# A decoder layer on one core: PSUM as four single banks and two pairs, with small products in groups of a pair

## The chip, the cores and the metric

The kernel runs on one core of one Trainium2 chip. The metric is the device time of one execution in microseconds (us), as the median of several runs. The engines are TensorE (PE; its weight loads are PEld), VectorE (DVE), ScalarE (ACT), GpSimd (POOL) and SyncE (SP), which here only issues DMAs. TensorE writes its results into PSUM, eight banks of 512 fp32 columns on each of 128 partitions; VectorE and ScalarE read them from there.

## The reference

One layer of a decoder works on x, 256 tokens of width 2048, in fp32:

```python
x = x + 0.5 * swiglu(rms_norm(x, g1), w_gate1, w_up1, w_down1)      # width 5632
p = rms_norm(x, g) @ w_in
# sliding-window attention: 16 heads of 64 in 4 key groups, blocks of 128 tokens
s = where(valid, (q @ k.T) * 64 ** -0.5, -1e30)
m = maximum(max(s, -1), sink)
e = exp(s - m)
y_attn = (e / (sum(e, -1) + exp(sink - m))) @ v
# RWKV-7: 16 heads of 64, a recurrence over the tokens, on p and p shifted by one token
y_rwkv = rwkv7_time_mix(p_rwkv, ...)
x = x + (gate_a * (y_attn @ w_proj_attn) + gate_r * (y_rwkv @ w_proj_rwkv)) @ w_out
x = x + softmax(q2 @ km.T * 128 ** -0.5) @ vm @ w_cross_o           # 4 heads, 256 memory rows
x = x + 0.5 * swiglu(rms_norm(x, g2), w_gate2, w_up2, w_down2)
out = rms_norm(x, g_final)
```

## The kernel before

**Weights and products.** A weight matrix comes from memory in pieces of 512 KB (128 partitions x 1024 columns, two blocks of 128 rows). `split_raw` (L315) makes two fp32r parts of each piece: `hi`, a cast on ScalarE (L321), and `lo`, the rest, a subtraction on VectorE (L322). The activations are split in the same way. `times` (L406) makes one product of a weight block as three products of 128x128 by 512 columns, one after the other, into one bank: hi by hi (L409), lo by hi (L410), hi by lo (L411). `product` (L387) runs these over all blocks for the two halves of the tokens. w_in has 17 column blocks of 512 and one of 288, whose pieces are 128x576 and whose products are 288 columns wide.

**Seven products.** In the feed-forward nets `product_pair` (L467) works two column blocks of 512 for both halves of the tokens. For some of the row blocks (SEVEN, SEVEN_DOWN) it makes them with seven products, p1 to p7, in place of eight, from sums of weights (`sums`, L334: first operation L341, then the parts thi at L346 and tlo at L347) and sums of activations (`combinations`, L421). For the others it uses p2, p4, p3 and p5 (p8 in w_down) as plain accumulators. `gate_up` (L526) and `down` (L557) give what is done when a sum is complete: `after(b)` reads p1, `end(b)` reads p6, p7 and p5 (L534 to L536), `finish` reads p2, p4, p3 and p5 (L542 to L550; p3 and p5 by the line L549). `gate_up` is called 20 times, in groups that w_down follows.

**PSUM.** The eight banks are three pools of tiles: `acc` (three), `mm` (three) and `tr` (two), each tile one bank (L164 to L171). A tile is given out in the order in which the code asks for it; the next user of a bank waits until the last reader of the tile before it is done. Dependencies are tracked by tile.

**Small products.** Between weight products TensorE makes small ones of 64 to 128 rows: transposes by `feat` (L599: four of 128x128 into one bank, then a copy or split of 512 columns by `split`, L609 with the lines L611 and L612, `to_features`, L847, or `Norm.block`, L626), the scores, transposes and value products of attention, and the products of the recurrence in chunks of 128 tokens (`invert` L1206, `chain` L1290 with `masked` L1315, `finish` L1420).

**Attention.** `attend(kv, qb)` (L857) handles one key group and one block of 128 queries, so there are eight units. Each makes its scores in two mm banks (L179, `by_turns`), adds the bias (L874, two operations), takes the maximum (L881), does four exponentials (L891 for the sink, L893), four scalings (L901), the transposes (L907) in one tr bank for each key block of 128, with a copy (L910) of 512 columns each, and the products with the values (L915) in a tr bank, split at L922 and L923. In the second block the keys are 256 wide. At most two units run at a time.

**Cross attention.** After `look_up` (L1536) sixteen products (L1583) of the probabilities with the memory's values fill one tr bank for each two heads; each bank is split into `oc` (L611, L612), from which `product` goes on with w_cross_o.

**What sets the order.** The code asks for work in one order: weight products, with `bg.tick()` between them. At each tick the groups of background generators (`Interleave`: const, feat, attn with two at a time, ew, inverse, chain, norm, mem) go on to their next `yield`. A scheduler then orders the instructions of each engine by their dependencies and its own estimate of times, and `issue_after` ties some to the one before. Each engine runs its instructions strictly in the order that comes out.

## Time and profile before

| what | before |
|---|---|
| time, median of 3 runs (lowest to highest) | 2241.64 us (2241.28 to 2242.18) |
| the profiled execution: its time, its span | 2241.35 us, 2239.6 us |
| mean granted clock of TensorE | 0.998 |
| TensorE busy | 2222.0 us |
| VectorE busy, ScalarE busy, GpSimd busy | 1742.0, 1202.7, 135.2 us |
| memory traffic over the span | 194 GB/s |

How to read it: a row of the timeline is "start, duration, engine, line, operation, out<-in, count, [idle before <- what ended it]"; rows of the same kind that follow each other are merged, with their count. A row of a group is "line, engine, operation, out<-in, count | busy us, mean ns of one | idle us before, what ended it". A matmul's duration reaches from its start to its modelled end, and the next one starts earlier, so busy TensorE is not TensorE at its peak. A row of the waits is "engine, what waits, for what: us in total, times, longest us".

### The profile page before, as it was taken

The numbers are of one execution on the slowest core, as the hardware profiler recorded it, in microseconds if no ns is written. First come the engines' busy times: TensorE is split into PE (matmuls) and PEld (weight loads), VectorE is DVE, ScalarE is ACT, GpSimd is POOL, SyncE is SP. The second block draws the span as 40 slices with busy tenths as digits, with TensorE's granted clock in tenths as the row PEclk, the third lists the DMA queues.
The fourth block names the chain that finished last, engine by engine and source line by source line (L and its number), as shares of the span: only waits on it lengthen the run. The fifth ranks groups of instructions, "written<-read, shape, count | busy, mean of one in ns | idle before, by whom it ended". The sixth has DMA issues, their size and how long they took to land.

```text
span 2239.6 us, 28587 instructions
## 1 busy us (share of the span) xinstructions
PE 2222.0 (99%) x10780; PEld 1821.2 (81%) x10780; DVE 1742.0 (78%) x2110; ACT 1202.7 (54%) x1524; POOL 135.2 (6%) x189
## 2 busy tenths in 40 slices
PE   9999999999999999999999999999999999999998
PEld 7888888888888877788888888888888888888886
DVE  7988988898887577895465466557888888898987
ACT  6555555555556567544343446556555555554554
POOL 1000000000000000301410030001000000000002
PEclk9999999999999999999999999999999999999999
DMA  7566665566556545667432786557565655555664
GB/s 246 204 221 197 206 206 189 198 197 201 195 188 216 165 128 167 212 217 224 125 101 91 243 270 220 188 165 257 199 205 188 207 189 198 196 194 200 207 203 155
DMA packets 219834, 435.42 MB, mean 194 GB/s; under 512 B 13888, under 2 KB 16016, under 8 KB 219696
## 3 DMA queue, kind: packets, MB, share of 16 engines
q1 hardware_dynamic: 210768, 406.37, 54.5%
q0 software_dynamic: 8352, 26.44, 3.8%
q8 instruction: 84, 1.38, 0.2%
q10 hardware_dynamic: 576, 0.79, 0.1%
q14 instruction: 54, 0.44, 0.1%
HBM read 420.05 MB, written 13.50 MB: 194 GB/s over the span
## 4 chain that ended last, share of the span: by engine, by line
PE 92%; DVE 4%; DMA 2%; issue 1%; ACT 1%; SPq 0%; POOLq 0%; POOL 0%; ACTq 0%; DVEq 0%
PE acc L409 19%; PE acc L410 19%; PE acc L411 19%; PE mm L411 8%; PE mm L410 8%; PE mm L409 8%; PE tr L606 2%; PE tr L410 2%; PE tr L411 2%; PE tr L409 1%; DVE lo L322 1%; PE mm L179 1%; DMA raw<-in_ffn_w_up_dram 1%; PE tr L179 1%; PE tr L1230 1%
## 5 line engine op out<-in xcount | busy, mean ns | idle before, releaser
L321 ACT CAST hi<-raw 128x1024 fp32r<-128x1024 f32 (+1 forms) x770 | 763.8, 1001 | 798.8 <-PE acc L411 401.3
L322 DVE TENSOR_TENSOR lo<-raw,hi 128x1024 fp32r<-128x1024 f32 (+1 forms) x770 | 892.3, 1170 | 345.6 <-ACT hi L321 344.1
L409 PE MATMUL acc<-hi,xhi 128*128 128x512 f32 (+1 forms) x1196 | 472.1, 395 | 2.6 <-ACT hi L321 2.2
L410 PE MATMUL acc<-lo,xhi 128*128 128x512 f32 (+1 forms) x1196 | 466.0, 390 | 1.3 <-DVE lo L322 1.2
L411 PE MATMUL acc<-hi,xlo 128*128 128x512 f32 (+1 forms) x1196 | 465.9, 390 | 0.0
L409 PEld LDWEIGHTS acc<-hi,xhi 128*128 128x128 f32 x1196 | 224.8, 188 | 52.9 <-issue 4.5
L410 PEld LDWEIGHTS acc<-lo,xhi 128*128 128x128 f32 x1196 | 225.2, 188 | 48.5 <-DVE lo L322 3.1
L411 PEld LDWEIGHTS acc<-hi,xlo 128*128 128x128 f32 x1196 | 225.0, 188 | 47.6 <-issue 1.7
L346 ACT CAST thi<-raw 128x1024 fp32r<-128x1024 f32 x160 | 165.9, 1051 | 70.3 <-DVE raw L341 34.7
L347 DVE TENSOR_TENSOR tlo<-raw,thi 128x1024 fp32r<-128x1024 f32 x160 | 193.4, 1222 | 1.3 <-ACT thi L346 1.3
L410 PE MATMUL acc<-lo,hhi 128*128 128x512 f32 x404 | 158.0, 391 | 0.0
L411 PE MATMUL acc<-hi,hlo 128*128 128x512 f32 x404 | 157.8, 391 | 0.0
L409 PE MATMUL acc<-hi,hhi 128*128 128x512 f32 x404 | 157.3, 392 | 0.0
L409 PE MATMUL mm<-hi,xhi 128*128 128x512 f32 x380 | 149.2, 393 | 0.0
L411 PE MATMUL mm<-hi,xlo 128*128 128x512 f32 x380 | 148.1, 390 | 0.0
L410 PE MATMUL mm<-lo,xhi 128*128 128x512 f32 x380 | 148.1, 390 | 0.0
L341 DVE TENSOR_TENSOR raw<-raw 128x1024 f32<-128x1024 f32 x80 | 98.0, 1225 | 22.9 <-DMA raw<-in_ffn_w_up_dram 21.3
L410 PEld LDWEIGHTS acc<-lo,hhi 128*128 128x128 f32 x404 | 75.9, 188 | 17.6 <-DVE lo L322 2.3
L409 PEld LDWEIGHTS acc<-hi,hhi 128*128 128x128 f32 x404 | 75.9, 188 | 16.1 <-DVE x L564 0.9
L411 PEld LDWEIGHTS acc<-hi,hlo 128*128 128x128 f32 x404 | 75.8, 188 | 15.3
L410 PEld LDWEIGHTS mm<-lo,xhi 128*128 128x128 f32 x380 | 71.4, 188 | 15.5 <-DVE lo L322 0.4
L411 PEld LDWEIGHTS mm<-hi,xlo 128*128 128x128 f32 x380 | 71.3, 188 | 14.7
(381 smaller groups left out, 3311.8 us busy)
## 6 DMA issues: line engine op xcount, KB each, us to landing
raw<-in_ffn_w_gate_dram SPq DMA_DIRECT2D x167, 512.0 KB, 3.7
raw<-in_ffn_w_up_dram SPq DMA_DIRECT2D x160, 512.0 KB, 4.6
raw<-in_ffn_w_down_dram SPq DMA_DIRECT2D x152, 512.0 KB, 4.7
raw<-in_w_in_dram SPq DMA_DIRECT2D x136, 512.0 KB, 3.5
raw<-in_w_out_dram SPq DMA_DIRECT2D x32, 512.0 KB, 4.3
raw<-in_ffn_w_down_dram SPq DMA_DIRECT2D x12, 1024.0 KB, 5.3
raw<-in_ffn_w_up_dram SPq DMA_DIRECT2D x8, 1024.0 KB, 7.4
raw<-in_w_proj_attn_dram SPq DMA_DIRECT2D x16, 512.0 KB, 3.5
```

What stands on the lines that cost most here:

```text
L179: prev = pe.matmul(*args, start=True, stop=True)
L321: newest["act"] = act.copy(hi[:, s], raw[:, s])
L322: newest["dve"] = dve.tensor_tensor(lo[:, s], raw[:, s], f32(hi[:, s]), ALU.subtract)
L341: dve.tensor_tensor(ta[:], raw[:, 1:3], raw[:, 0:2], ALU.subtract)
L346: act.copy(hi[:, s], t[:])
L347: dve.tensor_tensor(lo[:, s], t[:], f32(hi[:, s]), ALU.subtract)
L409: pe.matmul(o, xh, hi, start=first, stop=False, **how)
L410: pe.matmul(o, xh, lo, start=False, stop=False, **how)
L411: pe.matmul(o, xl, hi, start=False, stop=last, **how)
L606: pe.transpose(b[:, o : o + P], tok[:, t, col : col + P], ident[:])
L1230: pe.matmul(to, lhs, rhs, start=True, stop=True)
```

## The change

PSUM becomes four single banks (`acc`) and two pairs of banks (`two`, a tile of 2 x 512 columns). Every former user of `mm` and `tr` takes one or the other.

- `product_pair` puts p6 and p7 in one pair and p5 and p3 in another (PAIRS), the rest in single banks. `product` takes a pair for both token halves in one place (`paired`).
- `feats` in place of `feat`: eight transposes in a fixed order (`turn`, second token half first) into a pair, and one copy or split of 1024 columns, in the feed-forward nets, `to_features`, `merged` and `Norm.block`.
- `attend` takes two key groups for the first query block and one for the second, so there are six units. A unit's scores are one pair, with one operation for the bias; its eight transposes are one pair, last first, with one copy of 1024 columns; its value products are a single bank.
- `shifted` does four columns of blocks in one pass, with one copy for p and one subtraction on GpSimd (its tiles p and d have one buffer instead of two). `removal_keys`, `substitute`, `values`, `invert`, `masked`, `turned` and `finish` do with one operation over a pair what they did with two over single banks.
- `look_up` takes all four heads in one pair, with one maximum; the sixteen products of cross attention's output fill one pair, with one split of 1024 columns behind them.
- `memory` takes its tiles from another pool, and the four tiles x2 are asked for before w_out's products rather than one by one.

Lines move down a little: `times` is L418 to L420 in the new kernel, the splits of the weights L326 and L327, the transposes by `turn` L184, p3's and p5's reads L570, attention's scores L176, scalings L926, copy L937 and value products L943. The core of the diff:

```diff
@@ -162,13 +162,10 @@
         return x.bitcast(F32)
 
     def acc():
-        return ps.tile([P, 512], F32, tag="acc", name="acc")
-
-    def mm():
-        return ps.tile([P, 512], F32, tag="mm", name="mm")
-
-    def tr():
-        return ps.tile([P, 512], F32, tag="tr", name="tr", bufs=2)
+        return ps.tile([P, 512], F32, tag="acc", name="acc", bufs=4)[:]
+
+    def two():
+        return ps.tile([P, 2, 512], F32, tag="two", name="two", bufs=2)
 
     def by_turns(products):
 
@@ -178,6 +175,14 @@
             with tc.issue_after(prev.ins) if prev else nullcontext():
                 prev = pe.matmul(*args, start=True, stop=True)
 
+    def turn(blocks):
+
+
+        prev = None
+        for to, src in blocks:
+            with tc.issue_after(prev.ins) if prev else nullcontext():
+                prev = pe.transpose(to, src, ident[:])
+
     def wait_for(name):
...
@@ -473,12 +482,24 @@
         pw, _, nk, _, n = plan[at["product"]]
         assert pw[0].tensor is w.tensor and n == seven
         at["product"] += 1
-        b, begun, late = {e: bank[e]() for e in first}, set(), nk // KU - 1
+        b, begun, late = {}, set(), nk // KU - 1
+
+        def bank(to):
+            if to in b:
+                return
+            for pair in PAIRS:
+                if to in pair:
+                    banks = two()
+                    b.update((e, banks[:, i]) for i, e in enumerate(pair))
+                    return
+            b[to] = acc()
+
+        for e in first:
+            bank(e)
 
         def add(to, x_, w_, last):
-            if to not in b:
-                b[to] = bank[to]()
-            times(b[to][:], x_, w_, to not in begun, last, skip_group_check=True)
+            bank(to)
...
@@ -521,37 +542,37 @@
                     if t:
...
         )
 
-    def feat(tok, cols):
-
-
-        b = tr()
-        for i, col in enumerate(cols):
-            for t in range(2):
-                o = (2 * i + t) * P
-                pe.transpose(b[:, o : o + P], tok[:, t, col : col + P], ident[:])
-        return b[:].rearrange("p (c t) -> p c t", c=2)
+    def feats(tok, cols=(0, P, 2 * P, 3 * P)):
+
+
+        b = two()[:].rearrange("p a (c t) -> p (a c) t", t=T)
+        turn(
+            (b[:, i, t * P : (t + 1) * P], tok[:, t, col : col + P])
+            for t in (1, 0) for i, col in enumerate(cols)
+        )
+        return b[:, : len(cols)]
 
     def split(x: Act, c, n, src):
 
...
@@ -845,91 +864,103 @@
 
 
         def to_features(tok, dst, name):
-            for q in (0, 2):
-                act.copy(dst[:, q : q + 2, :], feat(tok, C4[q : q + 2]))
-                yield
+            act.copy(dst[:], feats(tok))
+            yield
             bg.seen.add(name)
 
         qt = []
         ya = act_tiles("ya", 2)
         sink4 = sinks[:].rearrange("p (k c e) -> p k e c", k=4, c=2)
 
-        def attend(kv, qb):
+        def attend(kvs, qb):
+
+
+
             yield from wait_for("kv")
-            yield from wait_for(f"q{kv // 2}")
-            w = P * (qb + 1)
+            yield from wait_for(f"q{kvs[0] // 2}")
+            w, nk = P * (qb + 1), len(kvs)
             tq = slice(qb * P, qb * P + P)
-            s = t4("s", (P, 2, 2, T))
-            b = [mm() for _ in range(2)]
+            s = t4("s", (P, 2, 2 * nk, w))
+            b = two()
             by_turns(
                 (
-                    b[e][:, c * w : (c + 1) * w],
+                    b[:, e, (2 * i + c) * w : (2 * i + c + 1) * w],
                     qt[kv // 2][64 * e : 64 * e + 64, 2 * (kv % 2) + c, tq],
                     kd[64 * e : 64 * e + 64, kv, :w],
                 )
-                for c in range(2) for e in (1, 0)
+                for i, kv in enumerate(kvs) for c in range(2) for e in (1, 0)
             )
             bias = abias[:, 1 - qb :, :].rearrange("p a b -> p (a b)")
-            for e in range(2):
-                dve.scalar_tensor_tensor(
-                    s[:, e, :, :w], b[e][:, : 2 * w].rearrange("p (c w) -> p c w", c=2), 0.125,
-                    bias.unsqueeze(1).to_broadcast([P, 2, w]), ALU.mult, ALU.add,
-                )
-            yield
             s3 = s[:].rearrange("p e c w -> p (e c) w")
-            m = stat.tile([P, 4], F32, tag="m", name="m")
-            dve.tensor_reduce(m[:], s3[:, :, :w], AX.X, ALU.max)
-            sk = sink4[:, kv]
-            m22 = m[:].rearrange("p (e c) -> p e c", e=2)
-            dve.tensor_tensor(m22, m22, sk, ALU.max)
-            nm = stat.tile([P, 4], F32, tag="nm", name="nm")
+            n = 4 * nk
+            dve.scalar_tensor_tensor(
+                s3, b[:].rearrange("p e (c w) -> p (e c) w", w=w), 0.125,
+                bias.unsqueeze(1).to_broadcast([P, n, w]), ALU.mult, ALU.add,
+            )
+            yield
+
+            def each(name):
+                return stat.tile([P, n], F32, tag=name, name=name)
+
+            def by_head(v):
+                return v[:].rearrange("p (e k c) -> p k e c", e=2, k=nk)
+
+            m, nm, es, den = (each(name) for name in ("m", "nm", "es", "den"))
+            dve.tensor_reduce(m[:], s3, AX.X, ALU.max)
+            for i, kv in enumerate(kvs):
+                mi = by_head(m)[:, i]
+                dve.tensor_tensor(mi, mi, sink4[:, kv], ALU.max)
+                dve.tensor_tensor(by_head(es)[:, i], sink4[:, kv], mi, ALU.subtract)
             dve.tensor_scalar(nm[:], m[:], -1.0, None, ALU.mult)
-            es = stat.tile([P, 4], F32, tag="es", name="es")
-            dve.tensor_tensor(es[:].rearrange("p (e c) -> p e c", e=2), sk, m22, ALU.subtract)
-            yield
-            den = stat.tile([P, 4], F32, tag="den", name="den")
+            yield
             act.activation(es[:], es[:], AF.Exp)
-            for i in range(4):
+            for i in range(n):
                 act.activation(
-                    s3[:, i, :w], s3[:, i, :w], AF.Exp, bias=nm[:, i : i + 1],
+                    s3[:, i], s3[:, i], AF.Exp, bias=nm[:, i : i + 1],
                     accum_out=den[:, i : i + 1],
                 )
             yield
             dve.tensor_tensor(den[:], den[:], es[:], ALU.add)
             dve.reciprocal(den[:], den[:])
-            for i in range(4):
-                dve.tensor_scalar(s3[:, i, :w], s3[:, i, :w], den[:, i : i + 1], None, ALU.mult)
+            for i in range(n):
+                dve.tensor_scalar(s3[:, i], s3[:, i], den[:, i : i + 1], None, ALU.mult)
             yield
             pt = t4("pt", (P, 2, 4, P))
-            for kb in range(qb + 1):
-                b = tr()
-                for i in range(4):
-                    pe.transpose(
-                        b[:, i * P : (i + 1) * P], s3[:, i, kb * P : (kb + 1) * P], ident[:]
-                    )
-                act.copy(pt[:, kb], b[:].rearrange("p (i q) -> p i q", i=4))
-            yield
-            b = tr()
-            for kb in range(qb + 1):
+            b = two()
+            turn(
+                (
+                    b[:, o, (2 * e + c) * P : (2 * e + c + 1) * P],
+                    s[:, e, c, o * P : o * P + P] if qb else s[:, e, 2 * o + c],
+                )
+                for e in (1, 0) for o in (1, 0) for c in (1, 0)
+            )
+            act.copy(pt[:].rearrange("p o i q -> p o (i q)"), b[:])
+            yield
+            b = acc()
+            for o in range(2):
+                i, kb = (0, o) if qb else (o, 0)
                 for e in range(2):
                     pe.matmul(
-                        b[64 * e : 64 * e + 64, : 2 * P], vt[:, kb, kv * 64 : kv * 64 + 64],
-                        pt[:, kb, 2 * e : 2 * e + 2, :].rearrange("p c q -> p (c q)"),
-                        start=kb == 0, stop=kb == qb,
+                        b[64 * e : 64 * e + 64, 2 * i * P : 2 * (i + 1) * P],
+                        vt[:, kb, kvs[i] * 64 : kvs[i] * 64 + 64],
+                        pt[:, o, 2 * e : 2 * e + 2, :].rearrange("p c q -> p (c q)"),
+                        start=o == 0, stop=i == 1 or kb == 1 or not qb, skip_group_check=True,
                     )
-            b3 = b[:, : 2 * P].rearrange("p (c q) -> p c q", c=2)
-            hi, lo = (ya.at(p, 2 * kv, 2)[:, :, tq] for p in range(2))
+            n = 2 * nk
+            b3 = b[:, : n * P].rearrange("p (c q) -> p c q", c=n)
+            hi, lo = (ya.at(p, 2 * kvs[0], n)[:, :, tq] for p in range(2))
             act.copy(hi, b3)
             dve.tensor_tensor(lo, b3, f32(hi), ALU.subtract)
             if qb:
-                ya.done |= {2 * kv, 2 * kv + 1}
-            if kv == 3 and qb:
+                ya.done |= {2 * kvs[0], 2 * kvs[0] + 1}
+            if kvs[0] == 3:
                 bg.seen.add("attn")
...
 
         def spawn_attention():
-            for kv in range(4):
-                for qb in range(2):
-                    bg.spawn("attn", attend(kv, qb))
+            for k in (0, 2):
+                bg.spawn("attn", attend((k, k + 1), 0))
+                for kv in (k, k + 1):
+                    bg.spawn("attn", attend((kv,), 1))
 
         kd = t4("kd")
         vt = t4("vt", (P, 2, KV_W))
...
@@ -1315,19 +1342,19 @@
             def masked(c, m):
                 x1, x2 = ((kh, ah), (kh, rh), (bh, rh))[m]
                 t = mk[c, m] = room("mk", (P, 2, 4, P))
-                b = [tr() for _ in range(2)]
+                b = two()
                 by_turns(
-                    (b[e][:, at(j)], x1[rows[e], j, at(c)], x2[rows[e], j, at(c)])
+                    (b[:, e, at(j)], x1[rows[e], j, at(c)], x2[rows[e], j, at(c)])
                     for j in range(4) for e in (1, 0)
                 )
-                for e in range(2):
-                    dve.tensor_tensor(
-                        t[:, e], b[e][:].rearrange("p (j t) -> p j t", j=4),
-                        mask3[:, m].unsqueeze(1).to_broadcast([P, 4, P]), ALU.mult,
-                    )
+                dve.tensor_tensor(
+                    t[:].rearrange("p e j t -> p (e j) t"),
+                    b[:].rearrange("p e (j t) -> p (e j) t", j=4),
+                    mask3[:, m].unsqueeze(1).to_broadcast([P, 8, P]), ALU.mult,
+                )
...
         oc = act_tiles("oc", 1)
-        for h in (0, 2):
-            b = tr()
-            for i in range(2):
-                for mb in range(2):
-                    pe.matmul(
-                        b[:, i * T : (i + 1) * T], vm[:, mb, (h + i) * P : (h + i + 1) * P],
-                        pt[mb][:, h + i, :], start=mb == 0, stop=mb == 1,
-                    )
-            split(oc, h, 2, b[:].rearrange("p (c t) -> p c t", c=2))
+        b4 = two()[:].rearrange("p a (h t) -> p (a h) t", h=2)
+        for h in range(4):
+            for mb in range(2):
+                pe.matmul(
+                    b4[:, h], vm[:, mb, h * P : (h + 1) * P], pt[mb][:, h, :],
+                    start=mb == 0, stop=mb == 1,
+                )
+        split(oc, 0, 4, b4)
         n4 = Norm(g_ffn2)
         for n in range(4):
             po = product(oc, W["w_cross_o"])
             for t in range(2):
-                dve.tensor_tensor(x2[n][:, t, :], po[t][:], x2[n][:, t, :], ALU.add)
+                dve.tensor_tensor(x2[n][:, t, :], po[t], x2[n][:, t, :], ALU.add)
             pool.dma_start(blk(x3d, n), x2[n][:])
```

335 lines of the change are left out of this document (161 added, 174 removed).

## The prediction

> **What bounds the kernel now.** I read the page first: busy times, the clock, the chain that ended last, and the two groups of casts that feed the products.
>
> ```profile
> span 2239.6 us, 28587 instructions
> PE 2222.0 (99%) x10780; PEld 1821.2 (81%) x10780; DVE 1742.0 (78%) x2110; ACT 1202.7 (54%) x1524; POOL 135.2 (6%) x189
> PEclk9999999999999999999999999999999999999999
> PE 92%; DVE 4%; DMA 2%; issue 1%; ACT 1%; SPq 0%; POOLq 0%; POOL 0%; ACTq 0%; DVEq 0%
> L321 ACT CAST hi<-raw 128x1024 fp32r<-128x1024 f32 (+1 forms) x770 | 763.8, 1001 | 798.8 <-PE acc L411 401.3
> L322 DVE TENSOR_TENSOR lo<-raw,hi 128x1024 fp32r<-128x1024 f32 (+1 forms) x770 | 892.3, 1170 | 345.6 <-ACT hi L321 344.1
> ```
>
> TensorE is busy 2222.0 of 2239.6 us at full clock and is 92% of the chain. VectorE is idle for a fifth of the span and ScalarE for almost half. So time saved on those two is worth nothing by itself; only what TensorE does or waits for counts. Next, its waits, and its busy time by stage (columns: stretch, length, PE, PEld, DVE, ACT, POOL, clock, DMA share, GB/s):
>
> ```profile
> PE acc L409 <- ACT hi L321: 2.2, 2, 1.2
> PE tr L410 <- DVE tlo L347: 1.9, 3, 1.0
> PE acc L410 <- DVE lo L322: 1.2, 2, 0.8
> PE mm L195 <- POOL ones L191: 1.1, 1, 1.1
> PE tr L907 <- DVE s L901: 0.7, 1, 0.7
> PE tr L915 <- ACT pt L910: 0.6, 1, 0.6
> PE mm L179 <- DVE lt L1106: 0.4, 1, 0.4
> ```
> ```profile
> 200.00:740.00 540.00, 539.62 (x2416) 444.44 (x2415) 464.53 (x532) 290.80 (x338) 4.71 (x8) 1.00 0.60 200
> 740.00:900.00 160.00, 158.05 (x834) 123.68 (x833) 110.67 (x194) 107.10 (x206) 11.07 (x15) 1.00 0.47 147
> 1085.00:1160.00 75.00, 75.00 (x858) 62.50 (x858) 39.68 (x53) 31.52 (x49) 18.02 (x31) 1.00 0.24 71
> 1400.00:1500.00 100.00, 99.77 (x466) 81.85 (x465) 54.63 (x71) 53.86 (x82) 2.15 (x3) 1.00 0.54 179
> ```
>
> There is little to win. The seven waits listed sum to 8.1 us, and 3.3 of them are the kernel's beginning (ones) and its first casts (hi). The first feed-forward net idles 0.38 us in 540; the recurrence, where most small products are, shows none in 75. Attention, inside 740 to 900, idles 1.95.
>
> **The small products themselves.** Here the first row is of attention's last unit; the second is cross attention's output.
>
> ```profile
> 827.93 1.14 PE L907 MATMUL tr<-ident,s 128*128 128x128 f32 x8 [0.66 <-DVE s L901]
> 829.63 1.57 PE L915 MATMUL tr<-pt,vt 128*64 128x256 f32 x12 [0.56 <-ACT pt L910]
> 1496.80 3.79 PE L1583 MATMUL tr<-ptm,vm 128*128 128x256 f32 x16
> 1500.25 0.58 PE L409 MATMUL acc<-hi,ochi 128*128 128x512 f32 x1
> ```
>
> The changed program has as many products as before (10117), with the same shapes. Eight transposes in one pair of banks are the same eight as in two banks, and eight in a row took 1.14 us, end to end: grouping takes nothing off TensorE. What goes is on the idle engines: 53 ACT copies, 49 VectorE operations on two tensors and 16 with a scalar (counted in the two programs); two ACT table loads are added (priced below). I value that at 0, since TensorE's own work lies over it; all DMAs stay, in number and queue. If that cover were gone, a copy of 1024 columns instead of two of 512 would save about 0.1 us (rows below). So the sum is made of waits alone: those that a larger piece lengthens and those that a free bank removes.
>
> The price of a wait comes from these rows (columns: start, duration):
>
> ```profile
> 821.90 0.29 PE L411 MATMUL acc<-hi,xlo 128*128 128x288 f32 x1
> 822.23 1.05 ACT L321 CAST hi<-raw 128x1024 fp32r<-128x1024 f32 x1 [0.54 <-PE acc L411]
> 828.99 1.07 ACT L910 COPY pt<-tr 128x512 f32<-128x512 f32 x2 [1.53 <-PE tr L907]
> L910 ACT COPY pt<-tr 128x512 f32<-128x512 f32 x12 | 6.6, 583 | 2.7 <-PE tr L907 2.6
> 775.60 1.28 ACT L893 ACT_TABLE_LOAD   x1
> ```
>
> ACT starts 0.04 us after the product ends (822.19, 822.23). A copy of 512 takes 0.58; one of 1024 I take at 1.05, the cast's time. The first copy ended at 829.57 and TensorE went on at 829.63, 0.06 later. A table load is 1.28 us; before, it lay under products, and I value the two added at 0 (2.6 if both stand in a chain that TensorE waits for).
>
> **1. Attention's last unit: +4.3 us.** With two key groups for the first query block, the last unit stands alone (one group, second block). In the changed order its last score product is followed by only 22 products of 288 columns, which finish w_in's column block of 288. Then come its eight transposes, in reversed order, so the first one waits for the last of four scalings. Queued behind that wait are the other seven, four value products and the whole next w_in product, whose bank comes after the unit's in the rotation. Before, 18 products of 512 columns of that next w_in product stood ahead of the transposes as well. The rows of one such unit before, and the width that covers it:
>
> ```profile
> 819.24 0.29 PE L409 MATMUL acc<-hi,xhi 128*128 128x288 f32 x1
> ...
> 820.01 1.28 DVE L874 SCALAR_TENSOR_TENSOR s<-mm,abias 128x512 f32<-128x512 f32 x2
> 821.33 1.22 DVE L881 TENSOR_REDUCE m<-s 128x4 f32<-128x1024 f32 x1
> 822.68 1.22 DVE L322 TENSOR_TENSOR lo<-raw,hi 128x1024 fp32r<-128x1024 f32 x1
> 824.83 0.19 ACT L891 ACTIVATE es<-es 128x4 f32<-128x4 f32 x1
> 826.40 0.49 ACT L893 ACTIVATE s<-s,nm 128x256 f32<-128x256 f32 x1
> 827.43 1.14 DVE L901 TENSOR_SCALAR s<-s,den 128x256 f32<-128x256 f32 x4
> ```
>
> From 819.24 to 821.90 there are 21 products of 288 columns, 0.133 us apart, so 22 cover 2.9 us. The chain over them: scaling and bias of 1024 columns 1.2, the reduce 1.2, one weight subtraction that stands between on VectorE 1.2, three small operations 0.5, then from the first small exponential to the end of the scalings 828.57 - 824.83 = 3.7, and 0.1 of releases: 7.9. TensorE stands for 7.9 - 2.9 = 5.0 us, where before it stood 0.66: **+4.3**. Bounds: 1.9 less if the subtraction is late enough to fall behind the small operations and the releases are shorter; 2 more if a second one falls in, or the copy before it holds ACT.
>
> The other five units have 7 to 11 us of products between scores and transposes against 8 to 12 of chain; those of the first half lie over 512-column products. The same count on before's units gives about the same deficit, so I take 0 for them, between -1.9 (all of attention's idle time goes) and +4 (the second pair of units, over 57 products of 288, 7.6 us plus four small ones, is late like the last).
>
> **2. Values behind one copy: +1.2 us.** In two units the value products directly follow their eight transposes. Before, they needed the first copy of 512 (829.63). Now: transposes end 829.07, copy 829.11 to 830.16, products 830.22: +0.59, twice. Bounds 0 and 2 x 1.2.
>
> [...]
>
> **3. Cross attention's output: +1.3 us.** All sixteen products now fill one pair and one cast of 1024 columns follows. They end at 1496.80 + 3.79 = 1500.59; cast 1500.63 to 1501.68; first product of w_cross_o at 1501.74, against 1500.25, of which 0.2 is taken as before's own wait for its second half: +1.3 (0.5 to 1.6). The six products then in front cover the subtraction of 1024 columns (1.23).
>
> **4. Product boundaries of the feed-forward nets: +1.5 us, and one in w_in: +0.9.** p3 and p5 now share a pair and tracking is by tile, so p5's last three products wait for VectorE's read of p3. Rows of one boundary before:
>
> ```profile
> 141.14 0.39 PE L411 MATMUL mm<-hi,xlo 128*128 128x512 f32 x1
> 141.36 0.39 PE L409 MATMUL mm<-hi,xhi 128*128 128x512 f32 x1
> 142.04 1.28 DVE L549 TENSOR_TENSOR u<-mm,u 128x512 f32<-128x512 f32 x2
> 146.83 1.22 DVE L341 TENSOR_TENSOR raw<-raw 128x1024 f32<-128x1024 f32 x1
> ```
>
> p3's last product starts at 141.14 and its read ends at about 142.72 (half of the two). The new order puts seven products of the next one (0.227 apart) in between: 141.14 + 8 x 0.227 = 142.96. The wait is hidden by 0.2 us, at 14 boundaries; 0. At the six boundaries into w_down a cast is released by a product only six places ahead: 0.39 + 0.04 + 1.05 + 0.06 = 1.54 of loop, against 1.36: with some restart, 0.25 each, +1.5. In w_in one has three places (0.68): 1.54 - 0.68 = +0.9. Bounds for all: 0 (the cast's operand is free earlier than the semaphore's product suggests) and +8 (rival A).
>
> **5. Waits that go: -1.2 us.** Triangle masks and recurrence copies in one piece now stand 3.7 to 5.5 us ahead of their users, instead of 0.9 to 1.4; scores no longer wait for a bank (0.4, L1106, and part of 1.95). I take -1.2, the end near the rows, since 1085 to 1160 shows no idle time; bounds 0 and -4 (with 1.9 of tlo).
>
> Sum: 4.3 + 1.2 + 1.3 + 1.5 + 0.9 - 1.2 = **+8.0**. The profiled execution took 2241.35 us (span 2239.6 and 1.75 around it), 0.29 below the median of 2241.64: 2241.35 + 8.0 = **2249.4 us**.
>
> **Rivals.**
>
> A. *Pairs hold TensorE at every boundary.* If VectorE reaches p3's or p5's read one 512-column operation later (0.6) at all 20, the 0.2 of slack turns into 0.4 each: +8 on top, 2257.4. For: VectorE works 464.53 of 540 us there, and the sums for the next product (L341) stand ahead of p5's read in the new order. Against: only one operation is moved.
>
> [...]
>
> B. *Not slower: the banks' freedom wins.* The mechanism is in the mixer alone: attention's last unit is covered (its chain under 3 us longer than its 2.9 of products, as before, when 0.66 was left) and the seven other attention and mixer waits vanish: -1.95 - 0.4 - 0.23 - 1.9 of tlo = -4.5: 2236.9. It decides at a stall under about 1 us in the last unit. Against: 3.7 us of the chain is four exponentials and four scalings, which nothing shortens.
>
> C. *It does nothing that can be measured.* Last unit stalls 2 or less, parts 2 to 5 cancel: 2241.4 + 1 = 2242.4. For: same products, all cuts on idle engines, and every wait rests on sub-microsecond slack.
>
> **How the numbers follow.** A measurement of this kernel tells about 0.2% (4.5 us) from no change: 2237.2 to 2246.1 is "same". Forecast 0.56 (its own range 2244 to 2254, with 0.04 of the 0.56 under 2246.1), A 0.14, C 0.21, B 0.09, of which 0.01 lies above 2237.2. Same is C, the forecast's 0.04 and B's 0.01, rounded to 0.25; slower 0.67, faster 0.08. The range runs from C's lower side, with part 5's bound, to A: 2238.5 to 2259.
>
> **What would show it.** Right: in attention's last unit TensorE waits some 5 us for a scaling, then over 1 us for pt; over 1 us before w_cross_o's first product; product and DMA counts unchanged; ACT and VectorE some 5 to 15 us less busy. Part 4: waits of 0.2 to 0.3 on hi at the start of w_down. Wrong: no wait above 2 us in attention (B or C), or p5's products waiting for the read of p3 at each boundary (A).

## The result, and the profile after

| | before | after |
|---|---|---|
| median (lowest to highest), 13 runs each | 2241.28 us (2239.84 to 2244.48) | 2248.26 us (2243.89 to 2250.59) |
| ratio to before, with its 95% interval | | 1.0029 (1.0020 to 1.0037) |
| span of the profiled execution | 2239.6 us | 2247.2 us |
| mean granted clock of TensorE | 0.998 | 0.995 |

The kernel became slower by 0.29%, 6.5 us. The forecast was 2249.4 us. The time is near it, but two of its terms were far off, in opposite directions, and one loss had no term at all; the experiments show which. The profile shows one execution of the 13: their clock lies between 0.995 and 0.998, and their time between 2243.89 us (0.998) and 2250.59 us (0.995).

The page of the changed kernel, the rows that answer to those of before:

```profile
span 2247.2 us, 28388 instructions
...
PE 2217.9 (99%) x10780; PEld 1821.7 (81%) x10780; DVE 1734.7 (77%) x2039; ACT 1201.1 (53%) x1467; POOL 129.1 (6%) x175
...
PEclk9999999999999999999999999999999999999999
...
PE 90%; DVE 5%; ACT 2%; DMA 2%; issue 1%; SPq 0%; POOL 0%; POOLq 0%; ACTq 0%; DVEq 0%
```

TensorE has as many products (10780 records in both traces) and is busy 4.1 us less, in a span that is 7.6 us longer. VectorE's and ScalarE's shares of the chain rose by a point each, though both work less. So waits came. TensorE's waits in the changed kernel:

```profile
PE acc L419 <- DVE lo L327: 6.5, 6, 3.2
PE two L184 <- DVE s L926: 5.4, 3, 5.0
PE acc L418 <- ACT hi L326: 2.2, 3, 0.8
PE acc L943 <- ACT pt L937: 2.2, 2, 1.1
PE two L184 <- DVE den L923: 1.4, 1, 1.4
PE acc L418 <- ACT ochi L632: 1.1, 1, 1.1
```

Two rows have a wait of more than 2 us: one for attention's scalings (5.0) and one for a weight subtraction (3.2). The list of before had none. Three of the stretches shown of before (columns: stretch, length, PE, PEld, DVE, ACT, POOL, clock, DMA share, GB/s):

```profile
200.00:740.00 540.00, 540.00 (x2420) 445.39 (x2419) 463.39 (x523) 291.75 (x333) 4.68 (x7) 1.00 0.63 200
740.00:900.00 160.00, 149.29 (x780) 117.86 (x779) 101.92 (x163) 104.57 (x187) 6.67 (x8) 0.97 0.47 136
1085.00:1160.00 75.00, 71.75 (x709) 59.50 (x707) 36.56 (x42) 30.08 (x40) 12.14 (x20) 1.00 0.25 69
```

The first feed-forward net has no idle time left (540.00 of 540). The stretch with attention went from 1.95 us idle to 10.71, and its clock from 1.00 to 0.97: a second loss that is no wait.

**Attention's last unit.** The timeline, from the subtraction that stands in the chain to the next long product: VectorE, then TensorE, then ScalarE.

```profile
821.57 1.23 DVE L327 TENSOR_TENSOR lo<-raw,hi 128x1024 fp32r<-128x1024 f32 x1
...
825.71 1.14 DVE L926 TENSOR_SCALAR s<-s,den 128x256 f32<-128x256 f32 x4
```
```profile
827.00 1.94 PE L184 MATMUL two<-ident,s 128*128 128x128 f32 x8 [4.96 <-DVE s L926]
830.04 1.97 PE L943 MATMUL acc<-pt,vt 128*64 128x256 f32 x8 [1.10 <-ACT pt L937]
831.95 0.80 PE L418 MATMUL acc<-hi,xhi 128*128 128x512 f32 x1
832.54 0.63 PE L419 MATMUL acc<-lo,xhi 128*128 128x512 f32 x1
832.97 0.63 PE L420 MATMUL acc<-hi,xlo 128*128 128x512 f32 x1
```
```profile
828.98 1.01 ACT L937 COPY pt<-two 128x1024 f32<-128x1024 f32 x1 [3.71 <-PE two L184]
```

The scalings end at 825.71 + 1.14 = 826.85 and TensorE waits 4.96 us for them, then 1.10 for the copy. Behind that, eight transposes take 1.94 us (1.14 before), and products of 512 columns start 0.43 us apart, not 0.227. The stretches show why:

```profile
822.00:827.00 5.00, 0.04 (x2) 0.03 (x1) 3.81 (x11) 3.19 (x10) 0.00 (x0) 0.78 0.53 133
827.00:834.00 7.00, 5.90 (x21) 3.97 (x22) 0.42 (x1) 2.18 (x4) 0.00 (x0) 0.50 0.14 55
834.00:836.00 2.00, 2.00 (x12) 1.61 (x11) 0.00 (x0) 0.30 (x1) 0.00 (x0) 0.75 0.03 8
```

The granted clock is 0.50 for 7 us behind the wait; by the trace's clock records it fell at 824.8, with 2.2 us of the wait to come, and rose again at 835.0. A page-wide row of 9s hides this.

**The recurrence's output.** The other long wait, on VectorE and TensorE:

```profile
1151.76 1.17 DVE L327 TENSOR_TENSOR lo<-raw,hi 128x1024 fp32r<-128x1024 f32 x1
1152.83 1.21 DVE L1469 TENSOR_TENSOR yq<-yq,sq 128x1024 f32<-128x1024 f32 x1
...
1158.63 1.22 DVE L327 TENSOR_TENSOR lo<-raw,hi 128x1024 fp32r<-128x1024 f32 x1
```
```profile
1159.90 0.80 PE L419 MATMUL acc<-lo,xhi 128*128 128x512 f32 x1 [3.25 <-DVE lo L327]
```

From the first of these subtractions to the second, VectorE works only for `finish` and for `receptances` (L1193): 5.8 us from 1152.83 to 1158.63. It isn't short of time on the whole; its order is bad at this place.

**Where the time is, by stage.** For every product of the trace I took the time from its start to the next one's start, less the usual distance for its shape (0.227 us for 512 columns, 0.133 for 288, a fixed value for each smaller width), and summed by stage. The table gives the difference to before, in us of the profiled execution. b1, c2 and d1 are experiments below, in which one, two and three costs are taken out of the changed kernel. The fixed values for the small widths decide how attention and the rest of w_in share their sum, by up to 2 us; the total doesn't depend on them. Some 1.7 us of the first row aren't the change's: the profiled executions of before (from 22.5 to 25.9 us) and of b1 (from 21.8 to 25.2) ran at half clock there, and those of after, c2 and d1 didn't.

| stage (us) | after | b1 | c2 | d1 |
|---|---|---|---|---|
| first feed-forward net, 0 to 750 | -1.9 | -0.3 | -1.7 | -2.1 |
| attention, 750 to 900 | +9.5 | -1.5 | -1.5 | -1.4 |
| rest of w_in, 900 to 1050 | -1.4 | -0.3 | -0.3 | -0.2 |
| recurrence, 1050 to 1250 | +1.6 | +0.4 | +1.5 | -4.1 |
| projections, 1250 to 1450 | -1.7 | -1.7 | -1.7 | -1.7 |
| cross attention, 1450 to 1550 | +1.2 | +1.3 | -0.5 | -0.5 |
| second feed-forward net | +0.1 | -0.9 | -0.5 | +0.7 |
| sum | +7.5 | -2.9 | -4.7 | -9.3 |
| difference of the spans | +7.6 | -2.9 | -4.5 | -9.3 |

### The profile page after: what moved, and what is told of

Its sections match the earlier page's. It is cut to its first block, busy times and chain, and to the rows that moved or that the text cites. A ratio compares the mean times of both kernels' runs of the same rounds, so it can differ in the third digit from the quotient of the medians.

```text
span 2247.2 us, 28388 instructions
## 1 busy us (share of the span) xinstructions
PE 2217.9 (99%) x10780; PEld 1821.7 (81%) x10780; DVE 1734.7 (77%) x2039; ACT 1201.1 (53%) x1467; POOL 129.1 (6%) x175
## 4 chain that ended last, share of the span: by engine, by line
PE 90%; DVE 5%; ACT 2%; DMA 2%; issue 1%; SPq 0%; POOL 0%; POOLq 0%; ACTq 0%; DVEq 0%
PE acc L418 20%; PE acc L419 20%; PE acc L420 19%; PE two L418 8%; PE two L419 8%; PE two L420 8%; PE two L184 2%; DVE lo L327 2%; DMA raw<-in_ffn_w_up_dram 1%; PE two L176 1%; DVE tlo L352 1%; ACT hi L326 0%; PE two L1258 0%; PE acc L1395 0%; PE acc L1377 0%
## 5 line engine op out<-in xcount | busy, mean ns | idle before, releaser
L326 ACT CAST hi<-raw 128x1024 fp32r<-128x1024 f32 (+1 forms) x770 | 763.8, 1001 | 801.6 <-PE acc L420 386.1
L327 DVE TENSOR_TENSOR lo<-raw,hi 128x1024 fp32r<-128x1024 f32 (+1 forms) x770 | 890.9, 1167 | 336.1 <-ACT hi L326 335.6
L419 PE MATMUL acc<-lo,xhi 128*128 128x512 f32 (+1 forms) x1256 | 489.2, 390 | 6.6 <-DVE lo L327 6.5
L418 PE MATMUL acc<-hi,xhi 128*128 128x512 f32 (+1 forms) x1256 | 492.7, 394 | 2.2 <-ACT hi L326 2.2
L420 PE MATMUL acc<-hi,xlo 128*128 128x512 f32 (+1 forms) x1256 | 488.2, 389 | 0.0
L419 PEld LDWEIGHTS acc<-lo,xhi 128*128 128x128 f32 x1256 | 236.8, 189 | 59.7 <-DVE lo L327 11.2
L418 PEld LDWEIGHTS acc<-hi,xhi 128*128 128x128 f32 x1256 | 236.4, 188 | 56.2 <-issue 4.4
L420 PEld LDWEIGHTS acc<-hi,xlo 128*128 128x128 f32 x1256 | 236.8, 189 | 48.2 <-issue 0.3
L351 ACT CAST thi<-raw 128x1024 fp32r<-128x1024 f32 x160 | 166.0, 1050 | 39.9 <-DVE raw L346 20.9
L420 PE MATMUL acc<-hi,hlo 128*128 128x512 f32 x424 | 165.2, 390 | 0.0
L418 PE MATMUL acc<-hi,hhi 128*128 128x512 f32 x424 | 159.9, 391 | 0.0
L418 PE MATMUL two<-hi,xhi 128*128 128x512 f32 x320 | 125.9, 394 | 0.1
L419 PE MATMUL two<-lo,xhi 128*128 128x512 f32 x320 | 124.7, 390 | 0.0
L420 PE MATMUL two<-hi,xlo 128*128 128x512 f32 x320 | 124.6, 389 | 0.0
L418 PEld LDWEIGHTS acc<-hi,hhi 128*128 128x128 f32 x424 | 79.1, 188 | 18.8 <-ACT hi L326 2.6
L420 PEld LDWEIGHTS acc<-hi,hlo 128*128 128x128 f32 x424 | 79.6, 188 | 16.2
L418 PEld LDWEIGHTS two<-hi,xhi 128*128 128x128 f32 x320 | 60.1, 188 | 13.8 <-DVE u L570 0.5
L418 PE MATMUL two<-thi,chi 128*128 128x512 f32 x180 | 70.3, 390 | 0.0
```

The costliest lines, as they stand in the source:

```text
L326: newest["act"] = act.copy(hi[:, s], raw[:, s])
L327: newest["dve"] = dve.tensor_tensor(lo[:, s], raw[:, s], f32(hi[:, s]), ALU.subtract)
L351: act.copy(hi[:, s], t[:])
L418: pe.matmul(o, xh, hi, start=first, stop=False, **how)
L419: pe.matmul(o, xh, lo, start=False, stop=False, **how)
L420: pe.matmul(o, xl, hi, start=False, stop=last, **how)
```

## The experiments

Theory R, after the result: the six units with their pairs leave attention's last unit without cover, and the order of the banks does it; cross attention's output costs a little; the rest is a gain. Rivals: the pairs as such cost (banks held too long), or the six units as such, or the two-key-group form. The kernels of each group (b, c, d) ran on one chip with runs of before, whose medians were 2241.61, 2241.89 and 2240.93 us. "Against before" is the ratio less one, times 2241 us.

| kernel | median us | ratio (95% interval) | against before |
|---|---|---|---|
| after | 2248.26 | 1.0029 (1.0020 to 1.0037) | +6.5 |
| b1 values in a pair | 2238.68 | 0.9987 (0.9978 to 0.9996) | -2.9 |
| b2 before, with six units | 2245.58 | 1.0014 (1.0006 to 1.0023) | +3.1 |
| b3 cross output in halves | 2246.67 | 1.0021 (1.0012 to 1.0030) | +4.7 |
| b4 key norms in halves | 2248.17 | 1.0027 (1.0018 to 1.0037) | +6.1 |
| c1 wait filled with products | 2242.72 | 1.0004 (0.9995 to 1.0013) | +0.9 |
| c2 = b1 and b3 | 2236.91 | 0.9979 (0.9970 to 0.9988) | -4.7 |
| c3 = c2 and b4 | 2236.95 | 0.9977 (0.9968 to 0.9986) | -5.2 |
| c4 after, with eight units | 2244.56 | 1.0008 (0.9999 to 1.0017) | +1.8 |
| d1 = c2, output spread | 2231.67 | 0.9960 (0.9948 to 0.9973) | -9.0 |
| d2 after, output spread | 2244.61 | 1.0014 (1.0005 to 1.0023) | +3.1 |

**b1: only the value products' bank.** One line of the changed kernel:

```diff
-            b = acc()
+            b = two()[:, 0]
             for o in range(2):
                 i, kb = (0, o) if qb else (o, 0)
```

> The changed kernel, with one line altered: attention's value products go into a bank of a pair instead of one of the four single banks. The changed kernel is 6.6 us above the one before. Theory R (rotation): the last unit stands alone because its value products' single bank comes ahead of the next w_in product's in the rotation, so that product cannot be moved ahead of the transposes. With the values in a pair, 33 products of 512 columns (7.5 us) stand between the last scores and the last transposes instead of 22 of 288 (2.9 us); the wait for the scaling falls from 5.0 to under 1 us and the values' copy is covered by 5 products: about +1 to +2.5 us over before. Theory U (units): six units with one-piece steps are too long for whatever stands beside them; the wait only moves, and the time stays at +5 to +7.

Measured: 9.4 us faster than after by the ratios, and 2.9 us faster than before, where R had said +1 to +2.5: the rest of the change gains more than R allowed for. The single bank for the values no longer stands between two weight products in the rotation of `acc`, so 33 products of 512 columns of the next w_in product run between the unit's scores and its transposes, in place of 22 of 288. Two rows of TensorE's timeline (b1), the last of these products and the transposes, and then the stretch with attention:

```profile
830.28 0.39 PE L420 MATMUL acc<-hi,xlo 128*128 128x512 f32 x1
830.92 1.06 PE L184 MATMUL two<-ident,s 128*128 128x128 f32 x8 [0.25 <-DVE s L926]
```
```profile
740.00:900.00 160.00, 155.54 (x844) 124.31 (x844) 110.04 (x173) 106.48 (x193) 11.02 (x10) 1.00 0.50 147
```

The chain over the unit is as long as before; it is covered. The wait is 0.25 us, the clock in 740 to 900 is 1.00, and the stage went from +9.5 to -1.5. R's cause is shown, and with the last unit covered the six units with their grouped products cost the stage nothing: the wait of 1.6 us for `den` is in its -1.5.

**b2: only the six units, in before.** The kernel before, its banks (`acc`, `mm`, `tr`) untouched, with `attend((k, k + 1), 0)` and single units for the second block; scores, transposes and copies of 512 columns as before.

> The kernel before, with attention's six units as the only change: two key groups for the first query block, in the old eight single banks, with transposes and copies by 512 columns. Theory R: without the new pools, 18 products of 512 columns of the next w_in product still stand ahead of the last unit's transposes (19 of 288 and 18 of 512, 6.6 us of cover against 7.9 of chain): at most +0.5 to +1.5 us over before. Theory U: +4 us or more over before, with a wait of some 4 to 5 us for the last unit's scalings.

Measured: +3.1 us, between the two theories. Two of TensorE's waits in b2:

```profile
PE tr L916 <- DVE s L909: 1.9, 1, 1.9
...
PE acc L409 <- DVE ga L1169: 1.7, 1, 1.7
```

Standing alone, the last unit costs something under the old banks too (1.9 us, against 0.66 with eight units), but less than the 5.0 in after, because 18 products of 512 and 19 of 288 cover it there. The other 1.7 us is a wait in another place, which this change of order brought.

**b3: cross attention's output in two single banks.**

```diff
-        b4 = two()[:].rearrange("p a (h t) -> p (a h) t", h=2)
-        for h in range(4):
...
-        split(oc, 0, 4, b4)
+        for h in (0, 2):
+            b = acc()
...
+            split(oc, h, 2, b.rearrange("p (c t) -> p c t", c=2))
```

> The changed kernel, with cross attention's output put back into two single banks with a split of 512 columns each. If the wait before w_cross_o's first product (1.1 us in the waits, 1.37 lost) is the one copy of 1024 columns: 1.0 to 1.4 us faster than the changed kernel, that is +5.2 to +5.6 over before, and the wait for ochi under 0.3. If it is only moved to the second half's lo part: +6.2 to +6.6.

Measured: 1.8 us less than after by the ratios. The intervals overlap, so the time alone doesn't show it; but the wait for `ochi` (1.1 us) is gone from the list, and cross attention's stage lost 1.8 us less. c2 shows the same.

**b4: the removal keys' norms in single banks.** `removal_keys` as before, two passes of 512 columns with two `acc` banks. The theory behind it (S) was that the late subtraction at 1159.9 comes from these norms' larger pieces.

> The changed kernel, with the norms of the removal keys put back: a product and a square root for each 512 columns into a single bank, then two reciprocals, instead of a pair and one square root of 1024. In the changed kernel TensorE waits 3.2 us for a weight subtraction (lo) at 1160 us and 0.7 for a cast (hi) at 921, neither of them before. Theory S (shift): these two come from the order in which VectorE's long operations of this stage fall since the key norms are one piece; then both waits go and the time is 3 to 4 us below the changed kernel: +2.5 to +3.5 over before. Theory F (finish): the subtraction at 1160 is late because of the two reciprocals of 3.35 us in the output stage, whatever the key norms do: +5.5 to +6.6.

Measured: no difference to after that can be told (+6.1 against +6.5). That lies in theory F's range, but what F said didn't happen: the subtraction is no longer late. The row for `lo` shrank as S said, and another came, at 905 us:

```profile
PE acc L419 <- DVE lo L327: 3.6, 6, 1.3
...
PE two L176 <- DVE kk L1110: 1.7, 1, 1.7
```

By the count of the table above, the recurrence in b4 takes 3 to 4 us less than in before, where after took 1.6 more. So S was right about this wait, and the time didn't follow: 1.7 us went into the wait for `kk`, and another 1.7 us or so into a stretch of half clock from 21.2 to 24.7 us in b4's profiled execution, which after's doesn't have.

**c1: the wait filled with products that nobody needs.** The changed kernel, with 20 products of 512 columns (4.5 us) ahead of the last unit's transposes, into the bank that the transposes then overwrite. The output is the same.

```diff
+            if kvs == (3,):
+                x2c = n2.x.at(0, 0, 2).rearrange("p c t -> p (c t)")
+                for i in range(20):
+                    pe.matmul(b[:, i % 2], n2.x.at(0, i % 16)[:, :P], x2c, start=True, stop=True)
```

> The changed kernel, with 20 products of 512 columns added that compute nothing that is used: they write into the last unit's pair of banks, ahead of its transposes, and are 4.5 us of useless work. In the changed kernel's trace the 5.0 us wait is followed by a granted clock of 0.50 until about 835 us, with products every 0.43 us instead of 0.227. Theory G (gate): the long wait costs twice, once itself and once by the half clock behind it, which is 3 to 4 us. With the wait filled to about 1 us (its length is set by the chain of 7.9 us, not by TensorE) the clock stays at 1.0 and the kernel is 3 to 5 us faster than the changed one although TensorE does more: +2 to +4 us over before. Theory N (no gate): the work fills the wait and gives nothing back, within 0.7 us of the changed kernel: +5.5 to +7.

Measured: with 4.5 us more work, 5.6 us faster than after. The stretch of c1 in which the transposes and the values' products stand:

```profile
825.00:830.00 5.00, 4.67 (x34) 3.65 (x34) 2.56 (x7) 3.46 (x5) 0.00 (x0) 1.00 0.14 20
```

The clock is 1.00. TensorE does work instead of waiting, so what is saved here isn't the wait but what came behind it: the half clock. Not all of the 5.6 us is that: six of the 288-column products now also stand between transposes and values and cover the copy, and in c1's profiled execution no half clock followed the other long wait either (3.2 us for `lo`; the clock was 1.00 from 1153 to 1160).

**c2: b1 and b3 together.**

> The changed kernel, with the value products in a pair and cross attention's output in two single banks. The first alone gave -2.9 us against before. If the two are independent, the wait for ochi (1.1 us) goes too: -3.8 to -4.5 us against before. If cross attention's output is hidden by nothing else (rival: the wait moves to the second half's lo part, as the 1.6 us of the run with that edit alone are within its noise): -2.5 to -3.2.

Measured: 11.2 us faster than after by the ratios, against 9.4 and 1.8 alone: the two add up. The wait for `lo` of 3.2 us stays, with the half clock behind it (a stretch of c2):

```profile
1150.00:1156.00 6.00, 5.80 (x14) 4.60 (x15) 4.16 (x6) 1.05 (x1) 0.00 (x0) 0.50 0.59 167
```

**c3: c2 with b4's edit.**

> As the kernel with the value products in a pair and cross attention in halves, and also the removal keys' norms put back to halves. With the last unit's wait gone, the wait of 3.2 us at the output stage (followed by 6 us at half clock) is the longest that is left. Putting the norms back removed it in the run with that edit alone, where others of 1.2 to 1.7 came in its place. Theory G: those are too short to lower the clock, so 3 to 5 us go: -7 to -9 against before. Rival: the new waits eat it, as they seemed to in that run: -3 to -5.

Measured: no difference to c2. As in b4, the wait of 3.2 us is gone, and the recurrence takes 3.7 us less than in before, where c2 took 1.5 more. Three losses stand against these 5.2 us in c3's profiled execution: 1.7 us of wait for `kk`, and two stretches of half clock of 3.4 us, some 1.6 us lost in each, at places where c2's clock is full. One is at 22.2, in the kernel's beginning; the other, at 817.5, comes behind a wait of 1.56 us for `den`, which c2 has too. So half clock followed a wait of that length once, which this expectation had called too short: over 800 to 840 the mean clock is 0.96 in c3 and 1.00 in c2. The norms do move the late subtraction, but by the medians putting them back gains nothing.

**c4: eight units in the changed kernel.** `attend` for one key group and one block, as before; scores in a pair, transposes and values in single banks.

> The changed kernel, with attention's eight units of before: one key group and one query block each, scores in a pair, transposes by four into a single bank with copies of 512 columns, value products in a single bank. Theory R (rotation of the single banks): the last units' transposes still stand ahead of the next w_in product, with 46 products of 288 columns (6.1 us) in front, against a chain of some 9 us for two units: a wait of 2 to 3 us, and +2 to +5 us over before. Theory U (the six wide units): with eight units attention is as before, and what is left of the change shows: -1 to +1.5.

Measured: +1.8 us, 4.7 less than after, and just outside both ranges. In c4 the scalings cost three shorter waits, 4.0 us in all; two of them stand close together (rows of TensorE's timeline, then a stretch of c4):

```profile
823.68 1.02 PE L926 MATMUL acc<-ident,s 128*128 128x128 f32 x4 [2.03 <-DVE s L920]
825.80 1.94 PE L926 MATMUL acc<-ident,s 128*128 128x128 f32 x8 [1.10 <-DVE s L920]
```
```profile
823.00:828.00 5.00, 2.96 (x12) 2.25 (x12) 3.67 (x12) 3.71 (x11) 0.00 (x0) 0.58 0.67 214
```

The clock fell here too: eight transposes took 1.94 us, as in after. Undoing the six units takes away most of the loss but not all of it, and less than b1's one line does with the six units kept. So neither the six units nor the two key groups are what costs.

**d1 and d2: only the order of VectorE in `finish`.** The late subtraction stood behind the operations of `finish` on one half of the recurrence's output. The edit gives the background two pauses ahead of them and two after each pair; the work is the same. d1 is this on c2, d2 on the changed kernel.

```diff
             dve.tensor_tensor(y[:], y[:], sq[:], ALU.mult)
...
+            yield from idle(2)
             for c in range(4):
...
                 if c % 2:
                     split(yr, 4 * h + c - 1, 2, y[:, c - 1 : c + 1])
-                    yield
+                yield from idle(2)
```

> The version with values and cross attention's output undone (c2), with two ticks of pause ahead of the eight normalising operations of each half of the recurrence's output, and two after each pair of them instead of one after each four. Nothing else is changed. The order that VectorE's instructions now have puts a weight subtraction (lo) after the third operation behind the normalisation's product, where it stood after the ninth. Theory O (the wait of 3.2 us for lo in this stage is VectorE's order alone, and the half clock behind it is the wait's): the wait falls to about 0.5 us or less, the half clock behind it goes, and the time falls against c2's 2236.9 by 3 us for the wait and about 2.6 for the clock: some 2231 (2230 to 2233.5). Rival F (as with the key norms in halves: VectorE is short of time here, and a subtraction that comes earlier lets another operation come late): another wait of 1.5 to 3 us in 1100 to 1250 takes its place, 2235 to 2238.

> The changed kernel with these pauses alone. Theory O: 3.2 us of the wait for lo and the 2.6 us of half clock behind it go: 2248.3 - 5.8 = 2242.5 (2241 to 2244.5), and the wait of 5.0 us in attention's last unit stays. Rival F: 2246.5 to 2249, with new waits in the recurrence's stage in place of the one that goes.

Measured: d1 2231.67 us, where theory O had said 2231. Rows of VectorE's timeline in d1, then TensorE's longest waits in d1:

```profile
1142.83 1.21 DVE L1469 TENSOR_TENSOR yq<-yq,sq 128x1024 f32<-128x1024 f32 x1
...
1145.15 1.21 DVE L327 TENSOR_TENSOR lo<-raw,hi 128x1024 fp32r<-128x1024 f32 x1
```
```profile
PE acc L418 <- ACT hi L326: 2.5, 3, 1.2
PE acc L419 <- DVE lo L327: 2.1, 3, 1.0
PE two L184 <- DVE den L923: 1.5, 1, 1.5
```

A subtraction comes 2.3 us after the normalisation's product began, where it came 5.8 after (1152.83, 1158.63). The wait is gone and, other than in b4 and c3, none took its place. d1 beats both kernels. d2 lies 3.4 us under after by the ratios, just above what O gave (2244.61 against at most 2244.5) and under F's 2246.5; its row for `lo` has 1.3 us at most, and the 5.0 us in attention stay:

```profile
PE two L184 <- DVE s L926: 5.4, 3, 5.0
PE acc L419 <- DVE lo L327: 2.9, 5, 1.3
```

In the spans of the profiled executions d2 gained 6.7 us (2247.2 to 2240.5). Its median gained less in part because that execution is the third shortest of d2's 11 (2240.1 to 2245.3), while after's is a little above the middle of its 13 (2242.2 to 2248.9).

## Why the prediction was right, and where it was wrong

**Right: the last unit (term 1), its mechanism and its wait.** Forecast: a chain of 7.9 us over 2.9 us of products, so 5.0 us of wait. The scores end at 818.93, the scalings at 826.85: 7.9; the wait is 4.96, against 0.66. One subtraction stands in the chain where it was placed. b1 shows that the place of the values' bank in the rotation is the reason.

**Wrong in size: what that wait costs.** The term had +4.3 us for the wait and nothing behind it. At half clock the eight transposes took 1.94 us instead of b1's 1.06, the eight value products 1.97 (the row at 830.04) instead of 1.08, and the six products from 831.95 to 834.67 took 2.72 instead of 6 x 0.227 = 1.36: together 3.1 us more. So in the profiled execution the wait cost about 7.4 us. Of the other five units, for which the sum had 0 with a bound of +4, one pair waits 1.4 us (`den`).

**Right: values behind one copy (term 2), cross attention's output (3).** Forecast +1.2: the waits for `pt` are 2.2 us, against 0.6. Forecast +1.3: 1.1 us of wait, in the last row below, and b3 got 1.8 back. The new w_in wait of term 4 (+0.9) is there too, in the first row: 0.68 of wait, and 0.96 of lost time by the starts, restart included. Rows of the changed kernel:

```profile
920.91 0.50 PE L418 MATMUL acc<-hi,xhi 128*128 128x512 f32 x1 [0.68 <-ACT hi L326]
...
1506.85 1.01 ACT L632 CAST ochi<-two 128x1024 fp32r<-128x1024 f32 x1 [2.44 <-PE two L1596]
...
1507.92 0.50 PE L418 MATMUL acc<-hi,ochi 128*128 128x512 f32 x1 [1.10 <-ACT ochi L632]
```

**Right: the feed-forward nets (4).** At each of the six boundaries into w_down a product comes late; one of them:

```profile
196.05 0.39 PE L420 MATMUL acc<-thi,hlo 128*128 128x512 f32 x1
196.46 0.73 PE L418 MATMUL acc<-hi,hhi 128*128 128x512 f32 x2
```

The distance is 0.41 instead of 0.227: 0.18 us late. The six are 0.16 to 0.18, together 1.0; the late product itself takes 0.11 us more than usual to the next start, which the forecast's 0.25 each counts in as restart. So the six come to 1.7 us, against 1.5. Too small for the list of waits, they show only in the distances. Of the other 14 boundaries two have a late product (0.5 and 0.3 us with the restart), where rival A had 0.4 at all 20: it is refuted.

**Wrong: the waits that go (5).** Forecast -1.2 us, bounds 0 and -4. With the three costs taken out, d1 is 9.0 us faster than before, with the 1.4 to 1.5 us for `den` and the late casts still in it. So the rest of the change is worth about nine us, not one. (d1's pauses are no part of the change, and weren't tried on before. But c2 has none, and comes to the same: its recurrence is 1.5 us above before's with 3.25 us of wait and 2.6 of half clock in it, so 4.4 below without these, where d1's is 4.1 below.) The step that failed is "grouping takes nothing off TensorE", and with it the reading of 1085 to 1160 as full because it was busy for 75.00 of 75. Busy time is modelled from start to end (0.39 us for a product of 512 columns whose next starts 0.227 later) and covers small gaps. In the recurrence, starts show 4.1 us less in d1 than in before: about 2.0 in its 192 products of 64 rows by 128 columns (15.14 us before, 13.10 in d1, from start to next start), about 1.7 at the changes between small groups and weight products, of which there are 30 instead of 38. One group of before, in two parts with a weight product between, and the same in d1, with the weight product that follows each:

```profile
1175.68 0.48 PE L179 MATMUL tr<-at,aa 64*128 64x128 f32 x2
1176.10 0.50 PE L409 MATMUL acc<-hi,xhi 128*128 128x512 f32 x1
1176.53 1.16 PE L179 MATMUL tr<-at,aa 64*128 64x128 f32 x14
1177.62 0.50 PE L410 MATMUL acc<-lo,xhi 128*128 128x512 f32 x1
```
```profile
1169.22 1.16 PE L176 MATMUL two<-at,aa 64*128 64x128 f32 x16
1170.31 0.50 PE L418 MATMUL acc<-hi,xhi 128*128 128x512 f32 x1
```

Before, start to start, 1177.62 - 1175.68 = 1.94 us, of which 0.23 is the weight product's usual distance: 1.71. In one piece it is 1170.31 - 1169.22 = 1.09. Over the whole program the changes from small products to weight products fell from 175 to 101 (106 in d1). How the nine us divide between such breaks and waits for banks outside the recurrence was not tried one by one.

**Not foreseen: the subtraction at 1159.9.** 3.25 us of wait, and 2.6 us of half clock behind it in the profiled execution (13 products at 0.43). The prediction counted what VectorE saves and not where its pieces stand. With the key norms in halves (b4, c3) it isn't late either, but the time stays; with nothing altered but the order in `finish` (d1, d2) the wait goes, and time with it: 4.3 us from c2 to d1 and 3.4 from after to d2, by the ratios. Why the scheduler put no subtraction there in the changed kernel stays open.

So +8.0 came near +6.5 because errors stood against each other: the nearness of the total is luck. Without terms 1 to 3 the sum has 8.0 - 4.3 - 1.2 - 1.3 = +1.2; d1, without their costs and the late subtraction, measured -9.0: some 10 us of gain were missed. Between d1 and after lie 15.5 us, where terms 1 to 3 have 6.8: some 9 us of loss were missed, 3.1 of them the half clock in attention and 5.9, by the profiled execution, the late subtraction with its own. Of the signs that it named, ScalarE's 5 to 15 us less failed: it is 1.6 less, VectorE 7.3. Rivals B and C needed a wait of under 1 and of at most 2 us in the last unit; 4.96 rules them out here. But b1, with that unit covered, is 2.9 us faster than before, so what B rested on, a gain from the free banks, is there. For a kernel like d1 the same reasoning as the forecast's would have named the wrong sign.

## What to carry to other kernels

Price a group of small products by two things: whether its result's chain is covered, for which the order in which tiles are asked for from a rotating set of banks decides (one line, which bank the values take, was worth 9.4 us), and how often it breaks the stream of long products, which busy time doesn't show but the distances of starts do. A wait of several us on TensorE can cost half clock as well (3.1 us behind the wait of 5.0, 2.6 behind one of 3.25), so a long wait can be worth filling even with useless products (c1, 5.6 us faster than after); waits in pieces close together didn't prevent it (c4: 2.03 and 1.10 us, and a clock of 0.58 from 823 to 828). When a change regroups work on a helper engine, look for the longest stretch without the piece that TensorE needs next, not at the engine's share.

## What the runs showed of the hardware

The half clock. Behind the wait of 4.96 us the clock was 0.50 from 827 to 834 and products of 512 columns came 0.43 us apart; with the wait filled (c1) it was 1.00 from 820 to 835. Some 5 us of wait was followed by half clock in the profiled executions of all four kernels that had it: 0.50 from 827 to 834 in after and d2, and from 828 to 835 in b3 and b4.

Behind the waits for `lo` of 3.2 to 3.3 us, in six kernels, a run of half-clock products followed directly in four (after 13 of them, b3 12, c2 13, c4 7) and in two not (b1, c1). The clock was 0.50 from 1160 to 1166 in after and from 1150 to 1156 in c2; its mean was 0.97 over 1085 to 1200 in b3 and 0.91 over 1150 to 1170 in c4; it was 1.00 from 1150 to 1158 in b1 and from 1153 to 1160 in c1. Behind a wait of 1.9 us (b2) none came (1.00 from 826 to 838); behind one of 2.03 with another of 1.10 two us later (c4) the clock was 0.58 from 823 to 828; behind one of 1.56 it was 0.50 for 3.4 us in c3 and 1.00 in c2. In b1 it was 0.50 from 1117.4 to 1120.9 behind small products of the recurrence, with no wait in the 3.4 us before.

By the clock records, half clock lasted 10.24 us in after at the wait of 4.96 (824.8 to 835.0, so until 8.0 us after the wait's end) and 6.83 at the one of 3.25 (1159.3 to 1166.1), and 3.41 in before (22.5 to 25.9). Why a wait of one length was followed by half clock in one kernel and not in another was not shown. So a wait's length alone didn't give its price in these runs, and each profile shows one execution.
